# A hybrid decoder step on one Trainium2 core: one of the seven products of the down projection is computed first instead of sixth

## The chip, the cores and the metric

The kernel runs on one core of one Trainium2 chip. The metric is the device time of one execution in microseconds (us). The engines are TensorE (PE, with its weight loads as PEld), VectorE (DVE), ScalarE (ACT), GpSimd (POOL) and SyncE (SP, whose queue issues most DMA transfers). Each engine works through its own queue in order.

## The reference, cut to what matters

One layer of a decoder trunk is computed for 1024 prompt tokens and 8 sample tokens: a gated delta rule, a sliding-window attention, two gates, an output projection, then a feed-forward part, then a last RMSNorm. Only the end of it matters here:

```python
gate = h2 @ lp['w_ffn_gate']
up = h2 @ lp['w_ffn_up']
...
gc = _causal_dwconv(gate_ext, lp['ffn_conv_w'], L) + lp['ffn_conv_b']
x = x + gt2 * ((jax.nn.silu(gc) * up) @ lp['w_ffn_down'])
...
y_prompt = _rmsnorm(xp, final_norm_w)
y_sample = _rmsnorm(xs, final_norm_w)
```

D_MODEL is 1024, D_FF 2816, and everything is float32.

## The kernel before, in words

A float32 product is made of three matmuls in a reduced format: each operand is split in a high and a low part, and `mm3` adds high x high, high x low and low x high (lines L180, L181, L182 in the profile). A split is one ACT instruction (L129, the high part) and one DVE subtraction (L130, the low part).

The down projection multiplies activations (2816 x 1032 tokens) with `w_ffn_down` (2816 x 1024). The method `ffn_down` takes both as 2 x 2 blocks and forms the result from seven block products instead of eight, in Strassen's way. Each product sums over G = 11 pairs of 128 rows; a (product, pair) is called a *step* here, and there are 77, numbered 0 to 76 in the order in which they are computed. A step has 8 tiles of 3 matmuls. Its activations, already added up in pairs, were stored to DRAM (`xd`) by the gate and up stage before. Its weights are made on the spot. The table `made` says how: products 5 and 2 need one 128 x 512 block of the weight (a *light* step), the other five need a sum or difference of two blocks (a *heavy* step). For a heavy step a second block is loaded into a `ws` buffer and POOL adds or subtracts it (L1754).

`fetch(s)` prepares step s: loads on SP's queue (L1750 the first block, L1753 the second, L1755 the activations) into one of five staging buffers (three named `raw`, two halves of `bmh0`), POOL's L1754 for a heavy step, then the split into one of 13 operand buffers. Their names run in the order of the list `tags`, so that steps 0, 13, 26, 39 stand in `bmh2`, steps 1, 14, 27, 40 in `bml0`, and so on. A staging buffer is free again when the DVE half of the split is done; an operand buffer when the matmuls of the step 13 places earlier are done. Fetches 18 to 23 also load a slice of the residual x (L1769).

After the last step of each product except the last product, its eight tiles are copied from their PSUM banks by ACT (`take`, L1782): a *block of copies*, six in all, behind steps 10, 21, 32, 43, 54 and 65. The next product's first matmul into a bank has to wait for that bank's copy. DVE then adds the copied tiles to x with a gate (`add_gated`, L1471, with L1475 and L1476 for the sample tokens): to two places each for products 5, 3, 1 and 2 (16 additions), to one for products 4 and 7 (8 additions), as the table `home` says. The last product, 6, goes tile by tile, and the final RMSNorm (`norm_rows`) is woven into it; it transposes finished columns of x on PE (L190) and squares them on ACT (L1865).

The order of the products is the tuple `chains`; products in one inner tuple share their PSUM accumulation. The program is emitted in this order and a scheduler then sets each engine's queue, by priorities and by its own estimate of times; the queues are fixed when the kernel runs.

Of the kernel before, what the change touches and what calls it, by code (L numbers as in the profile page):

```python
# [64 lines left out]
class Step:  # L65
# [1659 lines left out]
    def ffn_down(self, pool, psum):  # L1725
# [4 lines left out]
        made = {5: (2, (1, 1)), 3: (5, (0, 1), (1, 1), ALU.subtract), 4: (6, (1, 0), (0, 0), ALU.subtract),  # L1730
                7: (4, (1, 0), (1, 1), ALU.add), 1: (0, (0, 0), (1, 1), ALU.add), 2: (1, (0, 0)),
                6: (3, (0, 0), (0, 1), ALU.add)}
        chains = ((5, 3), (4, 7), (1,), (2,), (6,))
        home = {5: ((0, 0, -1), (1, 1, -1)), 3: ((1, 0, 1), (1, 1, 1)), 4: ((0, 1, 1),), 7: ((0, 0, 1),),
                1: ((0, 0, 1), (1, 1, 1)), 2: ((0, 1, 1), (1, 1, -1)), 6: ((1, 1, 1),)}
        steps = [(i, g) for c in chains for i in c for g in range(G)]
# [320 lines left out]
```

## Time and profile before

| | |
|---|---|
| runs shown | 2100.24, 2102.01, 4988.29 us (median 2102.01) |
| profiled execution | 2099.13 us, span 2097.4 us |
| mean granted TensorE clock | 0.983 |
| PE busy | 2027.4 us (97%) |
| DVE, ACT, POOL busy | 1362.2, 902.8, 520.2 us |
| DMA over the span | 275.75 MB, 131 GB/s |
| blocks of copies start at | 1880.7, 1912.2, 1950.5, 1984.6, 2014.6, 2046.2 us |

Times inside the execution count from the start of the span. The time from one block of copies to the next is called a stretch. In rows of a timeline a bracket at the end gives the idle time of the engine before the instruction and what ended it. In the table of stretches the columns are the busy times of PE, PEld, DVE, ACT and POOL with instruction counts, the granted TensorE clock, the DMA engines' busy share and GB/s.

### The profile page before, as it was taken

The numbers are of one execution on the slowest core, as the hardware profiler recorded it, in microseconds if no ns is written. First come the engines' busy times: TensorE is split into PE (matmuls) and PEld (weight loads), VectorE is DVE, ScalarE is ACT, GpSimd is POOL, SyncE is SP. The second block draws the span as 40 slices with busy tenths as digits, with TensorE's granted clock in tenths as the row PEclk, the third lists the DMA queues.
The fourth block names the chain that finished last, engine by engine and source line by source line (L and its number), as shares of the span: only waits on it lengthen the run. The fifth ranks groups of instructions, "written<-read, shape, count | busy, mean of one in ns | idle before, by whom it ended". The sixth has DMA issues, their size and how long they took to land.

```text
span 2097.4 us, 41330 instructions
## 1 busy us (share of the span) xinstructions
PE 2027.4 (97%) x16245; PEld 1924.1 (92%) x16245; DVE 1362.2 (65%) x2733; ACT 902.8 (43%) x2233; POOL 520.2 (25%) x594
## 2 busy tenths in 40 slices
PE   7999999999999999989999999999999999999998
PEld 3987778799999999989988999999999999999898
DVE  4756667564736647566554575479876776778875
ACT  3665545433333342442442452245544544544543
POOL 1000000021321211201211000004556556445530
PEclk8999999899999999999999999999999999999999
DMA  7246344152232312312266774413333333487972
GB/s 270 88 140 213 127 148 140 39 147 62 74 83 55 81 58 70 84 36 70 63 193 188 251 230 134 139 58 93 99 97 112 96 97 92 137 295 272 310 233 84
DMA packets 301887, 275.75 MB, mean 131 GB/s; under 512 B 59730, under 2 KB 248111, under 8 KB 301676
## 3 DMA queue, kind: packets, MB, share of 16 engines
q1 hardware_dynamic: 295852, 252.22, 39.2%
q0 software_dynamic: 5552, 20.37, 2.8%
q8 instruction: 127, 2.08, 0.4%
q14 instruction: 68, 0.56, 0.1%
q10 hardware_dynamic: 288, 0.52, 0.1%
HBM read 212.93 MB, written 62.51 MB: 131 GB/s over the span
## 4 chain that ended last, share of the span: by engine, by line
PE 77%; DMA 8%; DVE 6%; ACT 3%; issue 1%; SPq 1%; POOL 1%; DVEq 0%; POOLq 0%; ACTq 0%
PE mm L180 18%; PE mm L181 17%; PE mm L182 17%; PE wv L180 2%; PE wv L182 2%; PE wv L181 2%; PE pv L653 2%; DMA ws<-in_w_ffn_down_dram 1%; PE wy L180 1%; PE wy L182 1%; PE wy L181 1%; DMA raw<-in_w_ffn_down_dram 1%; PE pt L190 1%; PE tp L190 1%; PE sc L615 1%
## 5 line engine op out<-in xcount | busy, mean ns | idle before, releaser
L180 PE MATMUL mm<-b1h,wh 128*128 128x384 f32 (+1 forms) x1520 | 499.0, 330 | 4.9 <-ACT gt L1293 1.8
L181 PE MATMUL mm<-b1l,wh 128*128 128x384 f32 (+1 forms) x1520 | 491.0, 324 | 0.0
L182 PE MATMUL mm<-b1h,wl 128*128 128x384 f32 (+1 forms) x1520 | 490.6, 325 | 0.0
L180 PEld LDWEIGHTS mm<-b1h,wh 128*128 128x128 f32 x1520 | 287.9, 190 | 15.2 <-issue 5.8
L181 PEld LDWEIGHTS mm<-b1l,wh 128*128 128x128 f32 x1520 | 288.0, 190 | 5.4 <-issue 4.3
L182 PEld LDWEIGHTS mm<-b1h,wl 128*128 128x128 f32 x1520 | 287.3, 189 | 3.2 <-issue 2.3
L129 ACT ACTIVATE wh<-raw 128x1024 fp32r<-128x1024 f32 x83 | 87.0, 1048 | 118.5 <-PE mm L181 72.1
L130 DVE TENSOR_TENSOR wl<-raw,wh 128x1024 fp32r<-128x1024 f32 x82 | 101.2, 1235 | 53.6 <-ACT wh L129 52.5
L181 PE MATMUL mm<-pk,w 128*128 128x260 f32 (+1 forms) x440 | 124.9, 284 | 1.1 <-DVE pk L130 1.1
L180 PE MATMUL mm<-pk,w 128*128 128x260 f32 (+1 forms) x440 | 124.8, 284 | 0.0
L182 PE MATMUL mm<-pk,w 128*128 128x260 f32 (+1 forms) x440 | 124.6, 284 | 0.0
L130 DVE TENSOR_TENSOR w<-ws,w 128x512 fp32r<-128x512 f32 x88 | 79.4, 902 | 38.3 <-ACT w L129 38.1
L1625 ACT COPY bml<-mm 128x256 f32<-128x256 f32 (+1 forms) x132 | 48.9, 371 | 100.2 <-PE mm L182 97.1
L180 PE MATMUL mm<-bmh,w 128*128 128x260 f32 (+1 forms) x320 | 90.3, 282 | 0.0
L182 PE MATMUL mm<-bmh,w 128*128 128x260 f32 (+1 forms) x320 | 90.1, 282 | 0.0
L1680 DVE SCALAR_TENSOR_TENSOR fa<-fz,fcw,fa 128x512 f32<-128x512 f32 x88 | 75.0, 873 | 18.3 <-ACT fa L1678 18.0
L180 PE MATMUL mm<-b2h,wh 128*128 128x384 f32 (+1 forms) x256 | 83.3, 328 | 2.5 <-ACT wh L129 2.1
L181 PEld LDWEIGHTS mm<-pk,w 128*128 128x128 f32 x440 | 83.3, 189 | 1.3 <-DVE pk L130 1.3
L181 PE MATMUL mm<-b2l,wh 128*128 128x384 f32 (+1 forms) x256 | 83.6, 327 | 0.4 <-DVE b2l L130 0.4
L180 PEld LDWEIGHTS mm<-pk,w 128*128 128x128 f32 x440 | 83.3, 189 | 0.2 <-ACT bml L1625 0.2
L182 PEld LDWEIGHTS mm<-pk,w 128*128 128x128 f32 x440 | 83.5, 190 | 0.0
L182 PE MATMUL mm<-b2h,wl 128*128 128x384 f32 (+1 forms) x256 | 82.7, 325 | 0.0
(649 smaller groups left out, 5920.6 us busy)
## 6 DMA issues: line engine op xcount, KB each, us to landing
raw<-in_w_in_dram SPq DMA_DIRECT2D x60, 512.0 KB, 4.0
ws<-in_w_ffn_down_dram SPq DMA_DIRECT2D x55, 256.0 KB, 5.4
raw<-xd SPq DMA_DIRECT2D x47, 258.0 KB, 5.3
raw<-in_w_ffn_down_dram SPq DMA_DIRECT2D x47, 256.0 KB, 4.2
raw<-in_w_ffn_gate_dram SPq DMA_DIRECT2D x22, 512.0 KB, 3.8
raw<-in_w_ffn_up_dram SPq DMA_DIRECT2D x22, 512.0 KB
qst<-in_w_mod_dram SPq DMA_DIRECT2D x16, 512.0 KB, 7.8
raw<-in_w_mod_dram SPq DMA_DIRECT2D x16, 512.0 KB, 6.2
```

Of the source, the lines that this page charges most:

```text
L129: self.nc.scalar.activation(hi, x, AF.Copy)
L130: (eng or self.nc.vector).tensor_tensor(lo, x, hi.bitcast(F32), op=ALU.subtract)
L180: mm(ps, whi, xhi, start=first, stop=False, **kw)
L181: mm(ps, whi, xlo, start=False, stop=False, **kw)
L182: self.last_mm = mm(ps, wlo, xhi, start=False, stop=last, **kw).ins
L190: self.nc.tensor.transpose(out, in_, self.ident[:p, :p])
L615: self.scored = nc.tensor.matmul(sc[:, r, 256 - w:256], q, KH[:, lo:lo + w], start=True, stop=False)
L653: nc.tensor.matmul(pv[64 * r:64 * r + 64], V[:, n - back, ch], ps[:, r::2, :], start=back == 0, stop=back == (n > 0))
L1625: self.last_copy = nc.scalar.copy(r[p, i], x[p])
L1680: nc.vector.scalar_tensor_tensor(ai[:, c:e], zi[:, j + c:j + e], col(j), ai[:, c:e], op0=ALU.mult, op1=ALU.add)
```

## The change

One line changes, the order of the products:

```diff
-        chains = ((5, 3), (4, 7), (1,), (2,), (6,))
+        chains = ((2,), (5, 3), (4, 7), (1,), (6,))
```

Product 2 formerly held steps 55 to 65 and now holds 0 to 10; products 5, 3, 4, 7 and 1 each come 11 steps later; product 6 stays last. Both light products now stand in front: steps 0 to 21 are light and 22 to 76 heavy. Before, steps 0 to 10 and 55 to 65 were light.

ACT, third block of copies (behind step 32). `mm`, `wv`, `wy` and `nr` are the PSUM banks. Before:

```order
L129 ACTIVATE bmh3_2912_22043<-bmh0_2910_22037 128x1028
L129 ACTIVATE bmh2_2914_22077<-bmh0_2910_22037 128x1028
L1782 COPY bml3_2336_15623<-mm_2885_21876 128x256
L1782 COPY bml3_2336_15623<-wv_2886_21877 128x260
L129 ACTIVATE bml0_2917_22112<-raw_2915_22106 128x1028
L1782 COPY bml3_2336_15623<-wy_2887_21878 128x256
L1782 COPY bml3_2336_15623<-mm_2888_21879 128x260
```

Now:

```order
L129 ACTIVATE bml0_2910_22091<-raw_2908_22085 128x1028
L129 ACTIVATE bml2_2914_22129<-raw_2912_22123 128x1028
L129 ACTIVATE bmh1_2918_22167<-raw_2916_22161 128x1028
L1782 COPY bml3_2336_15623<-mm_2840_21446 128x256
L1782 COPY bml3_2336_15623<-wv_2841_21447 128x260
L1782 COPY bml3_2336_15623<-wy_2842_21448 128x256
```

Before, the split of step 39 (`bmh2`) was the last one ahead of the copies and step 40's (`bml0`) stood between them; now the splits of steps 40, 41 and 42 (`bml0`, `bml2`, `bmh1`) stand ahead as well. The second block moved the same way (steps 27, 28 and 29 are now ahead of it), and so did the fourth (53, 54, 55). The first has step 16 ahead instead of 15; the fifth and sixth have the same steps ahead as before, 64 and 75.

POOL, the first weight differences of the down projection. Before:

```order
L1720 DMA xd_2197_14347<-r_2337_15624 128x5x260
L1754 TENSOR_TENSOR raw_2822_21113<-raw_2822_21113,ws_2823_21115 128x512
L1754 TENSOR_TENSOR raw_2825_21122<-raw_2825_21122,ws_2826_21124 128x512
L1765 TENSOR_SCALAR less_2809_21079<-mT_125 128x72
L1754 TENSOR_TENSOR bmh0_2828_21155<-bmh0_2828_21155,ws_2829_21157 128x512
L1754 TENSOR_TENSOR bmh0_2828_21155<-bmh0_2828_21155,ws_2831_21189 128x512
```

Now:

```order
L1720 DMA xd_2197_14347<-r_2337_15624 128x5x260
L1765 TENSOR_SCALAR less_2809_21079<-mT_125 128x72
L1754 TENSOR_TENSOR bmh0_2853_21471<-bmh0_2853_21471,ws_2854_21473 128x512
L1754 TENSOR_TENSOR bmh0_2853_21471<-bmh0_2853_21471,ws_2856_21506 128x512
L1754 TENSOR_TENSOR raw_2850_21461<-raw_2850_21461,ws_2851_21463 128x512
L1754 TENSOR_TENSOR raw_2858_21537<-raw_2858_21537,ws_2859_21539 128x512
```

Before, the first one was made for step 11 (`raw_2822`), then 12, 13, 14; now the first is for step 23 (half of `bmh0_2853`), then 24, 22, 25. On SP's queue the three `ws` loads that stand far ahead serve these steps.

DVE, behind the splits for the third block of copies; the names `x1_` are slices of x. Before:

```order
L130 TENSOR_TENSOR bmh3_2912_22043<-bmh0_2910_22037,bmh3_2912_22043 128x1028
L130 TENSOR_TENSOR bmh2_2914_22077<-bmh0_2910_22037,bmh2_2914_22077 128x1028
L1471 SCALAR_TENSOR_TENSOR x1_0_2334_15618<-bml3_2336_15623,mT_125,x1_0_2334_15618 128x256
L1471 SCALAR_TENSOR_TENSOR x1_0_2334_15618<-bml3_2336_15623,mT_125,x1_0_2334_15618 128x252
L1475 TENSOR_TENSOR gtmp_2942_22399<-bml3_2336_15623,mT_125 128x8
L1476 TENSOR_TENSOR x1_0_2334_15618<-x1_0_2334_15618,gtmp_2942_22399 128x8
L130 TENSOR_TENSOR bml0_2917_22112<-raw_2915_22106,bml0_2917_22112 128x1028
```

Now:

```order
L130 TENSOR_TENSOR bmh1_2918_22167<-raw_2916_22161,bmh1_2918_22167 128x1028
L1471 SCALAR_TENSOR_TENSOR x1_4_2812_21083<-bml3_2336_15623,mT_125,x1_4_2812_21083 128x256 x2
L1471 SCALAR_TENSOR_TENSOR x1_4_2812_21083<-bml3_2336_15623,mT_125,x1_4_2812_21083 128x260
L1471 SCALAR_TENSOR_TENSOR x1_4_2812_21083<-bml3_2336_15623,mT_125,x1_4_2812_21083 128x252
L1475 TENSOR_TENSOR gtmp_2954_22525<-bml3_2336_15623,mT_125 128x8
L1471 SCALAR_TENSOR_TENSOR x1_5_2787_21033<-bml3_2336_15623,mT_125,x1_5_2787_21033 128x256 x2
L1471 SCALAR_TENSOR_TENSOR x1_5_2787_21033<-bml3_2336_15623,mT_125,x1_5_2787_21033 128x260
```

Before, eight additions of product 4 follow here, with splits between them; now sixteen of product 3 follow (a row with x2 stands for two) ahead of the next split.

## The prediction

> **What bounds the kernel now.** I read the page's first table, then the stretches of the down projection, then the timelines of PE, ACT and DVE there.
>
> ```profile
> PE 2027.4 (97%) x16245; PEld 1924.1 (92%) x16245; DVE 1362.2 (65%) x2733; ACT 902.8 (43%) x2233; POOL 520.2 (25%) x594
> ```
>
> PE works 97% of the span, so an edit that leaves its matmuls alone can only win or lose the idle time of PE where the edit acts. In the stretches below (from one block of eight copies to the next; columns PE, PEld, DVE, ACT, POOL, granted clock, DMA share, GB/s) PE has idle time in one place, between 1943.5 and 1950.4, and loses clock behind it.
>
> ```profile
> 1881.00:1912.00 31.00, 31.00 (x263) 31.00 (x262) 25.68 (x35) 13.86 (x19) 18.20 (x11) 1.00 0.90 317
> 1912.00:1943.50 31.50, 31.50 (x266) 31.50 (x266) 28.54 (x35) 13.12 (x18) 17.42 (x11) 1.00 0.76 259
> 1943.50:1950.40 6.90, 2.59 (x22) 2.38 (x20) 4.75 (x3) 3.04 (x3) 3.77 (x4) 0.93 1.00 350
> 1950.40:1984.60 34.20, 33.73 (x263) 33.73 (x264) 26.25 (x29) 15.96 (x22) 20.67 (x13) 0.91 0.91 305
> 1984.60:2014.60 30.00, 29.82 (x249) 29.40 (x248) 20.77 (x22) 14.61 (x21) 6.10 (x4) 1.00 0.77 256
> 2014.60:2046.20 31.60, 31.60 (x268) 31.60 (x267) 25.42 (x35) 14.29 (x20) 17.35 (x9) 1.00 0.65 216
> ```
>
> ```profile
> 1945.69 0.28 PE L181 MATMUL nr<-pk 128*128 128x260 f32 x1
> 1945.81 0.28 PE L182 MATMUL nr<-pk 128*128 128x260 f32 x1
> 1950.87 0.58 PE L180 MATMUL mm<-pk 128*128 128x256 f32 x1 [4.78 <-ACT bml L1782]
> 1951.25 0.41 PE L181 MATMUL mm<-pk 128*128 128x256 f32 x1
> 1951.46 0.41 PE L182 MATMUL mm<-pk 128*128 128x256 f32 x1
> ...
> 1988.52 0.39 PE L180 MATMUL wy<-bml 128*128 128x260 f32 x1 [0.15 <-ACT bml L1782]
> ```
>
> Matmuls start 0.12 us apart, so a product (264 of them) takes 31.2 us of PE. The stall of 4.78 us stands between the third and the fourth product and waits for ACT's copy of the first bank. Afterwards starts are 0.21 apart until 1956.2, some 26 of them: 26 x 0.097 = 2.5 us more. This boundary costs 7.3 us; the next one costs about 0.5 with its slow first matmuls.
>
> Why was ACT late? Its rows show it:
>
> ```profile
> 1880.73 0.37 ACT L1782 COPY bml<-mm 128x256 f32<-128x256 f32 x1 [5.75 <-PE mm L182]
> ...
> 1881.76 1.06 ACT L129 ACTIVATE bmh<-raw 128x1028 fp32r<-128x1028 f32 x1
> ...
> 1910.90 1.07 ACT L129 ACTIVATE bmh<-raw 128x1028 fp32r<-128x1028 f32 x1 [1.17 <-POOL raw L1754]
> 1912.19 0.37 ACT L1782 COPY bml<-mm 128x256 f32<-128x256 f32 x1 [0.23 <-PE mm L182]
> ...
> 1939.26 1.06 ACT L129 ACTIVATE pk<-raw 128x1028 fp32r<-128x1028 f32 x1 [1.17 <-POOL raw L1754]
> 1941.49 1.07 ACT L129 ACTIVATE pk<-raw 128x1028 fp32r<-128x1028 f32 x1 [1.17 <-POOL raw L1754]
> 1943.73 1.07 ACT L129 ACTIVATE pk<-raw 128x1028 fp32r<-128x1028 f32 x1 [1.17 <-POOL raw L1754]
> 1946.02 1.06 ACT L129 ACTIVATE bmh<-bmh 128x1028 fp32r<-128x1028 f32 x1 [1.22 <-POOL bmh L1754]
> 1949.50 1.06 ACT L129 ACTIVATE bmh<-bmh 128x1028 fp32r<-128x1028 f32 x1 [2.41 <-POOL bmh L1754]
> 1950.46 0.35 ACT L1782 COPY bml<-mm 128x256 f32<-128x256 f32 x1
> ...
> 1983.63 1.07 ACT L129 ACTIVATE bmh<-raw 128x1028 fp32r<-128x1028 f32 x1 [1.19 <-POOL raw L1754]
> 1984.60 0.35 ACT L1782 COPY bml<-mm 128x256 f32<-128x256 f32 x1
> ...
> 2014.64 0.37 ACT L1782 COPY bml<-mm 128x256 f32<-128x256 f32 x1 [3.89 <-PE mm L182]
> ...
> 2043.85 1.06 ACT L129 ACTIVATE pk<-raw 128x1028 fp32r<-128x1028 f32 x1 [2.44 <-POOL raw L1754]
> 2046.18 0.37 ACT L1782 COPY bml<-mm 128x256 f32<-128x256 f32 x1 [1.27 <-PE mm L182]
> ```
>
> ACT works in order. The copies of step 32 stand behind the split of step 39, and that split waits for POOL's subtraction of two weight blocks. Heavy steps (two blocks) come at best every 2.24 us (1939.26, 1941.49, 1943.73, 1946.02). PE's 2.84 us a step would cover this, but DVE's additions to x1 come in one burst after each block of copies:
>
> ```profile
> 1886.08 5.33 DVE L1471 SCALAR_TENSOR_TENSOR x<-bml,less,x 128x256 f32<-128x256 f32 x8
> 1920.81 6.39 DVE L1471 SCALAR_TENSOR_TENSOR x<-bml,mT,x 128x256 f32<-128x256 f32 x8
> 2016.72 1.67 DVE L1471 SCALAR_TENSOR_TENSOR x<-bml,mT,x 128x256 f32<-128x256 f32 x4
> 2003.09 2.44 DVE L130 TENSOR_TENSOR pk<-raw,pk 128x1028 fp32r<-128x1028 f32 x2
> ```
>
> ```profile
> L1754 POOL TENSOR_TENSOR raw<-raw,ws x33: 1265/1471/3742, 1860.2 to 2044.2; 128x512 f32<-128x512 f32 x33
> ```
>
> One addition takes 0.42 us where POOL is quiet (2016.72) and 0.67 to 0.80 where POOL subtracts (1886.08, 1920.81); POOL's subtraction ranges from 1.27 to 3.74 us. The two slow each other, the five staging buffers stay full meanwhile, and loads stop. So a stretch is priced by its heavy steps and its additions:
> - 13 heavy splits and 16 additions, started without a reserve: 1912.19 to 1950.46, 38.3 us.
> - 11 heavy splits and 16 additions, started with full buffers: 1881.76 to 1911.97, 30.2 us.
> - 13 heavy and 8 additions: 1950.46 to 1984.60, 34.1 us.
> - 1 light, 10 heavy, 16 additions, with full buffers: 2014.64 to 2044.91, 30.3 us.
> A light split costs DVE 1.22 us (2003.09).
>
> The Trainium skill (SBUF — State Buffer, "Who interferes with whom") says that a VectorE instruction with two SBUF inputs and a GpSimd instruction that reads SBUF exclude each other for a whole instruction. By that rule heavy work and additions simply add up, which agrees with 0.80 against 0.42 us; it speaks against a change that puts heavy steps and additions together, as this one does between the third and the fourth block.
>
> **The change part by part.** Totals stay: 1848 matmuls, 55 heavy and 22 light steps, 48 copies, the same DMAs on SP's queue. What moves is 11 light steps, each with one 256 KB weight load and one load from xd, and each without a POOL subtraction, from places 55–65 to 0–10; the other light product goes from 0–10 to 11–21. POOL's first subtraction is then step 22's group, not step 11. Additions to x1 per stretch, formerly 16, 16, 8, 8, 16 in the five stretches between blocks, become 16, 16, 16, 8, 8, since the moved product has two destinations and so have products 5 and 3.
>
> *Up to the first block of copies:* PE never waits there now, and ACT idles 5.75 us before it. Lighter splits make that idle time longer. The lead cannot be kept, because ACT's next split stands behind the copies, as the built order has it: it has done step 16, formerly 15. Worth 0; with a cover of 5.75 us it also costs 0.
>
> *First to second block:* steps 17–29: 5 light, 8 heavy, 16 additions. From the row with full buffers: 30.2 - 3 x 2.24 + 5 x 1.22 = 29.6. From the one without: 38.3 - 5 x (2.24 - 1.22) = 33.2. PE gives 31.5, and since eight tiles are finished one behind the other, the first copy may be some 2.2 us late before PE waits. I take the middle, 31.4: no stall, and no reserve either. Ends: 0 and 1 us.
>
> *Second to third block:* steps 30–42: 13 heavy, 16 additions. Without a reserve 38.3, as in the row of the same count; with one 30.2 + 2 x 2.24 = 34.7. I take 38.3, since the stretch ahead leaves nothing over. That is the 7.3 us of before again: no difference. Ends: 34.7 would leave 1 us of stall, a gain of 6.3; one microsecond handed on from the stretch ahead costs 1.
>
> *Third to fourth block:* steps 43–55: 13 heavy and now 16 additions, not 8. 38.3 against 34.1: 4.2 us later than the one that just fitted. So PE stalls 4.2 us and loses another 2.5 to slow matmuls: +6.7. Ends: 34.7 is 0.6 late, which the 2.2 us of cover hides (0); a stretch that also finds DVE behind from the additions of the last one adds perhaps 3 (+9.7).
>
> The Trainium skill (TensorE: Matmul & The Clock Gate, "Part 1: The HAM clock gate") states that the slow clock comes after an idle window of about 3.4 us. The 4.78 us stall with slow starts and the 0.15 us one without agree; by the rule a stall under 3.4 us would cost its own length alone, here 4.2 + 2.5 stays, but a 2 us stall would cost 2, not 4.5.
>
> *Fourth to fifth:* 9 heavy, 8 additions: 34.1 - 4 x 2.24 = 25.1, under 31.2, no stall. The 0.5 us at the old fourth boundary is inside the +6.7. *Fifth to sixth:* 11 heavy, 8 additions: 34.1 - 2 x 2.24 = 29.6, under 31.2: no stall (end: 1).
>
> *The tail:* product 1's additions, now last, touch the first quarter of the tokens, which the final norm transposes first; product 2's did not.
>
> ```profile
> 2046.59 0.48 DVE L1471 SCALAR_TENSOR_TENSOR x<-bml,mT,x 128x256 f32<-128x256 f32 x1
> ...
> 2052.50 0.60 PE L190 MATMUL wv<-ident,x 128*128 128x128 f32 x4
> ```
>
> The thirteenth addition is the last that matters: 2046.59 + 13 x 0.42 = 2052.1, ahead of 2052.50, and its transpose was put 12 matmuls later. Worth 0, at worst 1.
>
> **Sum:** 0 + 0 + 0 + 6.7 + 0 + 0 = +6.7 us on the profiled 2099.13 (span 2097.4), 2105.8. The runs shown are 2100.24 and 2102.01 beside one of 4988; their middle, 2101.1, lies 2.0 above the profiled one, so I forecast 2108.
>
> **The rivals.** *The lead is kept* (not slower): if 29.6 holds in the first stretch, buffers are full at the second block, the next takes 34.7 and the third as well. The stall of 7.3 shrinks to about 1 and none follows: 2101.1 - 6.5 = 2095. For it: eleven early subtractions are gone, and DMA falls from 317 GB/s there. Against it: the five buffers hold light steps while DVE adds, so no heavy step is staged when the burst ends. *The stall only moves*: one of the two stretches runs at 35 and the other at 38.3; 2099 to 2103, say 2101. *A third stall* (slower): the first heavy loads start when DVE's burst ends near 1889, and 8 heavy steps at 2.9 us (38.3 / 13) need 24 us, to 1913 and beyond, with steps 17–21 between. This decides from 33.7 us on; the second block stalls 2 to 3 us, the next stretches inherit it: +6.7 + 3 + 5 = 2116. *No effect*: were copies not behind splits on ACT, order would not matter; the 4.78 us row speaks against it.
>
> **How the numbers follow.** Forecast, by itself 2104 to 2111 (+3 to +10 us): 0.38. Lead kept: 0.24. Moved only: 0.18. Third stall: 0.18. No effect: 0.02. The range reaches from 2095 (lead kept) to 2118 (third stall and the tail's 1). Faster or slower by over 2% (42 us, about what a measurement of this kernel can tell from no change) would take six stalls of 7 us, one at every boundary: 0.02 for slower; for faster there are only 8 us to win: 0.01.
>
> **What would show it.** Right: PE idle 4 to 6 us behind ACT L1782 at the third and the fourth boundary, each followed by starts 0.21 apart, none at the others; DVE bursts at 0.7 to 0.8 us an addition. Wrong: no stall at the third boundary (lead kept), or one at the second (third stall), or PE waiting in the tail for x1. ACT's idle time before the first copies must grow beyond 5.75 us.

## The result and the profile after

The changed kernel takes 2105.5 us (median of 15 runs, 2101.7 to 2109.78) beside 2100.19 us for the kernel before on the same chip (15 runs): the ratio is 1.0028, with a 95% interval of 1.002 to 1.0036. By the bound of 2% this is no change; as a difference of 0.3% it is resolved, and it is a loss. The forecast was 2108.0 us, with a range of 2095 to 2118. The profiled execution takes 2106.4 us, 7.3 more than that of before.

PE's timeline of the changed kernel has three waits of more than 0.3 us from the first block of copies to the end. (Columns: start, duration, instruction, and in brackets the idle time before it and what ended it.)

```profile
1949.44 0.58 PE L180 MATMUL mm<-pk 128*128 128x256 f32 x1 [4.72 <-ACT bml L1782]
1989.97 0.58 PE L180 MATMUL mm<-bml 128*128 128x256 f32 x1 [6.29 <-ACT bml L1782]
2096.20 0.80 PE L190 MATMUL wy<-ident,x 128*128 128x128 f32 x2 [0.98 <-ACT ws L1865]
```

The stall at the third boundary is still there, a second one stands at the fourth, and both wait for ACT's copy. The wait of 0.98 in the tail is the same as before. ACT's timeline gives the starts of the six blocks of copies, and here the split ahead of three of them:

```profile
1877.34 1.06 ACT L129 ACTIVATE bmh<-raw 128x1028 fp32r<-128x1028 f32 x1 [5.48 <-DMA raw<-xd]
1879.01 0.38 ACT L1782 COPY bml<-mm 128x256 f32<-128x256 f32 x1 [0.60 <-PE mm L182]
...
1912.50 0.35 ACT L1782 COPY bml<-mm 128x256 f32<-128x256 f32 x1
...
1948.07 1.06 ACT L129 ACTIVATE bmh<-raw 128x1028 fp32r<-128x1028 f32 x1 [0.17 <-POOL raw L1754]
1949.04 0.35 ACT L1782 COPY bml<-mm 128x256 f32<-128x256 f32 x1
...
1988.60 1.06 ACT L129 ACTIVATE bmh<-raw 128x1028 fp32r<-128x1028 f32 x1 [0.80 <-POOL raw L1754]
1989.56 0.35 ACT L1782 COPY bml<-mm 128x256 f32<-128x256 f32 x1
...
2021.89 0.37 ACT L1782 COPY bml<-mm 128x256 f32<-128x256 f32 x1 [4.95 <-PE mm L182]
...
2053.39 0.37 ACT L1782 COPY bml<-mm 128x256 f32<-128x256 f32 x1 [2.49 <-PE mm L182]
```

A bracket that names PE means that ACT was there first; the second, third and fourth block have no such bracket, so there ACT was late. At the third and fourth the copies start the moment the splits of steps 42 and 55 are done. The stretches are 33.5, 36.5, 40.5, 32.3 and 31.5 us long, where before they were 31.5, 38.3, 34.1, 30.0 and 31.5. In the table of stretches (columns as before) the 7 us ahead of both blocks have little PE work, a DMA share near 1, and the stretches behind them a granted clock near 0.92:

```profile
1879.00:1912.50 33.50, 33.50 (x283) 33.50 (x282) 28.24 (x45) 16.52 (x22) 14.21 (x8) 1.00 0.87 297
1912.50:1942.50 30.00, 30.00 (x251) 29.81 (x250) 27.50 (x35) 12.83 (x19) 19.42 (x11) 1.00 0.77 252
1942.50:1949.40 6.90, 2.23 (x19) 2.02 (x17) 4.60 (x4) 3.46 (x5) 3.60 (x3) 0.92 0.96 332
1949.40:1983.00 33.60, 33.56 (x260) 33.56 (x261) 28.81 (x35) 12.59 (x17) 22.94 (x11) 0.92 0.73 247
1983.00:1990.00 7.00, 0.71 (x7) 0.50 (x5) 4.67 (x4) 3.52 (x5) 4.50 (x4) 0.70 1.01 361
1990.00:2021.90 31.90, 31.90 (x245) 31.90 (x246) 22.79 (x26) 11.35 (x17) 17.95 (x12) 0.91 0.79 264
```

The balance of the two profiled executions: the first block starts 1.7 us earlier, from the first to the sixth it takes 174.4 us instead of 165.4, and from the sixth to the end 51.3 instead of 51.2. That is -1.7 + 9.0 + 0.1 = 7.3 us. Of the 9.0, stalls make 6.1 (11.0 instead of 4.9) and the second period of slow clock about 2.5.

The timeline of DVE in the burst behind the third block shows how additions go:

```profile
1950.31 2.70 DVE L1471 SCALAR_TENSOR_TENSOR x<-bml,mT,x 128x256 f32<-128x256 f32 x4
1952.93 0.15 DVE L1475 TENSOR_TENSOR gtmp<-bml,mT 128x8 f32<-128x8 f32 x1
1953.01 1.66 DVE L1471 SCALAR_TENSOR_TENSOR x<-bml,mT,x 128x256 f32<-128x256 f32 x4
...
1956.25 1.26 DVE L1476 TENSOR_TENSOR x<-x,gtmp 128x8 f32<-128x8 f32 x1
1957.44 1.66 DVE L1471 SCALAR_TENSOR_TENSOR x<-bml,mT,x 128x256 f32<-128x256 f32 x4
```

Most of them take 0.42 us (1.66 for four). Some instruction in between takes about 1.1 us more, and it need not be a large one: an addition of 128 x 8 values takes 0.15 us or 1.26.

### The profile page after: what moved, and what is told of

Read it like the earlier page. It is cut to its first block, busy times and chain, and to the rows that moved or that the text cites. A ratio compares the mean times of both kernels' runs of the same rounds, so it can differ in the third digit from the quotient of the medians.

```text
span 2104.7 us, 41320 instructions
## 1 busy us (share of the span) xinstructions
PE 2029.8 (96%) x16245; PEld 1926.4 (92%) x16245; DVE 1364.8 (65%) x2733; ACT 902.9 (43%) x2233; POOL 528.4 (25%) x594
## 4 chain that ended last, share of the span: by engine, by line
PE 78%; DMA 7%; DVE 7%; ACT 3%; issue 1%; SPq 1%; POOL 1%; DVEq 0%; POOLq 0%; ACTq 0%
PE mm L180 18%; PE mm L181 17%; PE mm L182 17%; PE wv L180 2%; PE wv L182 2%; PE wv L181 2%; PE wy L182 1%; PE wy L180 1%; PE wy L181 1%; PE pv L653 1%; PE tp L190 1%; PE mm L264 1%; PE pt L190 1%; PE tp L905 1%; PE tp L906 1%
## 5 line engine op out<-in xcount | busy, mean ns | idle before, releaser
L130 DVE TENSOR_TENSOR wl<-raw,wh 128x1024 fp32r<-128x1024 f32 x82 | 101.5, 1238 | 53.7 <-ACT wh L129 52.7
L130 DVE TENSOR_TENSOR w<-ws,w 128x512 fp32r<-128x512 f32 x88 | 79.8, 907 | 38.0 <-ACT w L129 37.9
```

The source lines that it names most:

```text
L130: (eng or self.nc.vector).tensor_tensor(lo, x, hi.bitcast(F32), op=ALU.subtract)
```

## The experiments

The **theory** was that the copies are late because they stand on ACT behind splits of steps far ahead, and that those splits are late because heavy steps and additions share the time of a stretch (theory A: DVE and POOL exclude each other). **Rivals**: PE's operands are late in any case; the loads set the pace (theory B); the burst of additions starves the loads (theory C). Times below stand against the kernel before, run on the same chip.

**1. Fewer splits ahead of the copies.** In both kernels,

```diff
-                        fetch_to(s + len(tags))
+                        fetch_to(s + len(tags) if s >= 55 else min(s + len(tags), s - g + G + 7))
```

On the changed kernel:

> The changed kernel with one more edit: up to step 54 the splits may run at most six steps past the end of the product being computed, not ten, so that on ACT the copies of the third block stand behind the split of step 39 and those of the fourth behind step 50, not 42 and 55. The computation is the same. Theory (the copies are late only because they queue on ACT behind splits that are far ahead and late): the stalls of 4.72 and 6.29 us at the third and fourth block both vanish, and with them about 2 x 2.5 us of slow clock; time about 2105.5 - 16 = 2090 us, and every block but the first starts 31.2 to 32 us after the one before. Rival (the operands themselves are late): the two stalls go from the bank's copy to the operands of the next product (PE waits for a split, at some step behind the boundary), and the time stays at 2102 to 2106.

Measured: 2098.56 us, ratio 1.0007 (0.9996 to 1.0018). ACT's timeline for the third and fourth block, and PE's waits:

```profile
1940.72 0.35 ACT L1782 COPY bml<-mm 128x256 f32<-128x256 f32 x1
1972.71 0.35 ACT L1782 COPY bml<-mm 128x256 f32<-128x256 f32 x1
```

```profile
2007.47 0.39 PE L180 MATMUL mm<-bmh 128*128 128x256 f32 x1 [1.81 <-ACT bml L1782]
2045.87 0.58 PE L180 MATMUL mm<-bml 128*128 128x260 f32 x1 [6.61 <-ACT bml L1782]
```

The stretches up to the fourth block are 31.4, 31.8 and 32.0 us: with 11 or 12 splits in a stretch both stalls are gone, and no operand was late in their place. So the wait is the place of the copies in ACT's queue; the first rival falls. The gain, by the ratios 0.2% or 4 us where I expected 15, is mostly lost again at the sixth block: the limit ends at step 55, so that 14 heavy splits stand between the fifth and the sixth, 38.4 us and a stall of 6.61. The fifth block, 1.81 us late, I had not expected: 11 heavy splits and 8 additions in 34.4 us. The loads had paused there behind the burst (the row has a DMA share of 0.16), and ACT then waited for POOL, which waited for its loads.

```profile
1982.00:1987.00 5.00, 5.00 (x44) 5.00 (x43) 4.78 (x5) 1.07 (x1) 5.00 (x2) 1.00 0.16 59
```

On the kernel before:

> The same limit of six steps on the kernel before (order 5, 3, 4, 7, 1, 2, 6). Theory: its one stall (4.78 us with 2.5 of slow clock) vanishes, about 2100.2 - 7 = 2093 us, and it then differs from the limited changed kernel by less than 3 us: without copies behind late splits the order of the products hardly matters. Rival (operands late): no gain, 2098 to 2101, and the changed order with the limit stays about 5 us slower than this one.

Measured: 2097.96 us, ratio 1.0003 (0.9991 to 1.0014), and the stall at the third boundary stayed (5.13 us, stretch 38.6). This was a slip of mine: the kernel before has the split of step 39 ahead of the third block anyway, and 26 ahead of the second, so the limit left 13 heavy splits in that stretch. It fits the theory, but tests nothing.

**2. Other places for the light steps.**

```diff
-        chains = ((2,), (5, 3), (4, 7), (1,), (6,))
+        chains = ((5, 3), (2,), (4, 7), (1,), (6,))
```

> The order 5, 3, 2, 4, 7, 1, 6: the light product 2 third, no other edit. Light steps are then 0 to 10 and 22 to 32; stretches hold 5 heavy + 8 light steps with 16 additions, 3 light + 10 heavy with 16, 13 heavy with 16, 9 heavy with 8, 11 heavy with 8. Theory (a stretch is priced by its heavy steps and additions): the second block is on time, the third is up to 2 us late (no more than a short stall), the fourth is the late one (13 heavy + 16 additions, 36.5 to 40.5 us by the two such stretches of the changed kernel) and stalls 3 to 7 us; time 2097 to 2103. Rival (the place of the third block as such is late, whatever steps stand there): a stall of 4 to 5 us at the third block.

Measured: 2098.98 us, ratio 1.0008 (0.9997 to 1.0018); stalls of 1.63 at the third and 5.96 at the fourth boundary, stretches of 31.8, 34.9, 37.7, 32.0 and 31.5. All as the theory had it.

```diff
-        chains = ((2,), (5, 3), (4, 7), (1,), (6,))
+        chains = ((4, 7), (5, 3), (2,), (1,), (6,))
```

> The order 4, 7, 5, 3, 2, 1, 6: light steps are 22 to 32 and 44 to 54, so that they are split where DVE has 16 additions, and heavy ones where it has 8. Stretches: 5 heavy + 8 light with 8 additions, 3 light + 10 heavy with 8, 2 heavy + 11 light with 16, 9 heavy with 16, 11 heavy with 16. Theory: no stall at the second to the sixth block, which saves the 7.3 us of the kernel before; but the first two products are heavy, so POOL has 17 subtractions to make before the first block, where it still adds up activations: this may cost 0 to 10 us at the beginning of the down projection. Time 2093 to 2103. Rival (the load traffic paces the heavy steps, not their sharing with additions): a stall of 4 us or more at the third block, since there the 10 heavy steps also need two loads each.

Measured: 2098.2 us, ratio 1.0007 (0.9994 to 1.0021). Behind the first block every stretch is 31.4 or 31.5 us long, without a stall; PE's waits all stand before:

```profile
1845.43 0.39 PE L180 MATMUL mm<-pk,w 128*128 128x256 f32 x1 [1.21 <-ACT bml L1625]
1850.45 0.39 PE L180 MATMUL wv<-pk,w 128*128 128x256 f32 x1 [1.66 <-DVE bml L1700]
1888.73 0.58 PE L180 MATMUL mm<-pk 128*128 128x256 f32 x1 [5.60 <-ACT bml L1782]
```

Light steps among the additions keep the stretches in time, as the theory prices them, and heavy steps in front cost their time ahead of the first block: the three waits add up to 8.5 us, and the kernel before has none of them.

```diff
-        chains = ((2,), (5, 3), (4, 7), (1,), (6,))
+        chains = ((5, 3), (1,), (2,), (4, 7), (6,))
```

> The order 5, 3, 1, 2, 4, 7, 6: light steps are 0 to 10 and 33 to 43; stretches hold 13 heavy steps with 16 additions (started with full buffers), 3 heavy + 10 light with 16, 1 light + 12 heavy with 16 (started with full buffers again), 9 heavy with 16, 11 heavy with 8. Theory (a stretch is late only where about 13 heavy steps meet 16 additions without a light product before them): no stall at any block, each block 31.2 to 32 us after the one before, time of the kernel before less 7.3, about 2091 us, the ratio 0.996 to 0.9975. Rival (whichever stretch first has 13 heavy steps and 16 additions is late): a stall of 4 us or more at the second block or at the fourth, and a time of 2096 to 2101.

Measured: 2105.35 us, ratio 1.0037 (1.0025 to 1.005), and stalls at the third and the fifth boundary:

```profile
1948.88 0.58 PE L180 MATMUL mm<-pk 128*128 128x256 f32 x1 [5.05 <-ACT bml L1782]
2019.72 0.58 PE L180 MATMUL mm<-bmh 128*128 128x256 f32 x1 [5.46 <-ACT bml L1782]
```

My expectation failed, and the rival's places were wrong too. I had counted the steps of each stretch as they are in the changed kernel. The queue of this order has 16 splits between the second and the third block (steps 27 to 42: 6 heavy, 10 light; 38.6 us) and 13 heavy ones between the fourth and the fifth (steps 54 to 66, with 16 additions; 38.9 us). PE uses up 11 steps in a stretch. How many splits the queue puts between two blocks matters as much as how heavy they are.

The first of these two stretches also shows a second way to be late, which the price by heavy steps and additions does not cover. POOL's last subtraction in it ends at 1924.1 and DVE's burst at 1925.1. The loads had stood still behind the burst (a DMA share of 0.20 in the row), ACT then idled 8.05 us for activations, and nine of the ten light splits waited for a load:

```profile
1925.00:1930.00 5.00, 5.00 (x44) 5.00 (x44) 5.00 (x10) 0.18 (x1) 0.00 (x0) 1.00 0.20 62
1933.23 1.07 ACT L129 ACTIVATE pk<-bmh 128x1028 fp32r<-128x1028 f32 x1 [8.05 <-DMA bmh<-xd]
```

**3. Taking away one cost at a time** in the stretch between the third and the fourth block. Additions first:

```diff
-        home = {5: ((0, 0, -1), (1, 1, -1)), 3: ((1, 0, 1), (1, 1, 1)), 4: ((0, 1, 1),), 7: ((0, 0, 1),),
+        home = {5: ((0, 0, -1), (1, 1, -1)), 3: ((1, 1, 1),), 4: ((0, 1, 1),), 7: ((0, 0, 1),),
```

> The changed kernel with product 3 added to one place instead of two (its additions to the other quarter are left out): 8 additions instead of 16 in the stretch from the third to the fourth block, nothing else moved. Theory (additions and heavy steps share the time of the stretch): the stretch falls from 40.5 us to 34 to 36 us, the stall of 6.29 us at the fourth block to 0 to 2.5 us, and the time by 5 to 8 us to about 2098. Rival (loads alone pace the heavy steps): 13 heavy steps have the same loads, the stretch stays at 39 to 41 us and the stall above 5 us.

Then the loads (for product 7 POOL adds the two blocks; the texts call this a subtraction too):

```diff
-                other = self.t(self.pw, [P, 512], "ws", bufs=3)
-                nc.sync.dma_start(other, src[1])
+                other = raw[:, n:] if i == 7 else self.t(self.pw, [P, 512], "ws", bufs=3)
+                if i != 7:
+                    nc.sync.dma_start(other, src[1])
```

> The changed kernel with the second weight load of product 7 (steps 44 to 54) left out; POOL still subtracts, a block from itself. Of the 13 heavy steps between the third and the fourth block 11 then load 514 KB instead of 770. Theory A (DVE and POOL in each other's way set the pace): the stretch stays at 39 to 41 us and the stall above 5 us. Theory B (the loads set the pace, 770 KB a step at about 350 GB/s being 2.2 us): 11 x 0.73 = 8 us less, the stretch falls to 32 or 33 us and the stall vanishes.

Then the subtractions:

```diff
-                nc.gpsimd.tensor_tensor(raw[:, n:], raw[:, n:], other, op=src[2])
+                if i != 7:
+                    nc.gpsimd.tensor_tensor(raw[:, n:], raw[:, n:], other, op=src[2])
```

> The changed kernel with POOL's subtraction for product 7 (steps 44 to 54) left out; both loads are still made. Theory A (DVE and POOL in each other's way): additions fall to 0.42 us throughout in that stretch, which ends 8 us or more sooner, 31 to 33 us, without a stall. Theory B (loads): the stretch stays at 38 to 41 us, since 770 KB are loaded for each step as before. Between them, 35 to 37 us: the burst of additions holds back the buffers and the loads have to catch up, so that both count.

One row of the stretches for each, in this order (columns as before):

```profile
1950.30:1985.20 34.90, 34.45 (x264) 34.25 (x264) 29.74 (x30) 15.88 (x22) 21.40 (x14) 0.91 0.87 306
```

```profile
1951.70:1986.70 35.00, 33.53 (x264) 33.32 (x264) 29.92 (x38) 15.83 (x23) 18.00 (x14) 0.94 0.64 215
```

```profile
1952.00:1983.80 31.80, 31.44 (x251) 31.44 (x252) 24.44 (x38) 15.67 (x23) 2.86 (x3) 0.95 0.95 339
```

| left out | stretch | stall at the fourth boundary | median, ratio |
|---|---|---|---|
| nothing | 40.5 us | 6.29 us | 2105.5, 1.0028 (1.002 to 1.0036) |
| 8 additions | 35.0 | 0.51 | 2101.32, 1.0016 (1.0005 to 1.0026) |
| 11 second loads | 35.0 | 1.44 | 2103.78, 1.0031 (1.0019 to 1.0042) |
| 11 subtractions | 31.8 | below 0.3 | 2098.42, 1.0005 (0.9995 to 1.0014) |

With half the additions and without the subtractions the stretch came out as theory A had it (34 to 36 and 31 to 33 us) and not as B had it (38 us or more). Without the second loads it lies between the two: loads count (5.5 us, where B said 8), but with the DMA engines busy only 0.64 of the time the stretch is still 35 us long. So neither alone holds. Without the subtractions it falls to PE's pace with every load in place, and DVE's small additions (from 1952 to 1984 us, the changed kernel first; busy us and mean ns) are short:

```profile
L1476 DVE TENSOR_TENSOR x<-x,gtmp 128x8 f32<-128x8 f32 x4 | 2.8, 710 | 0.0
L1476 DVE TENSOR_TENSOR x<-x,gtmp 128x8 f32<-128x8 f32 x4 | 0.5, 148 | 0.0
```

The times fall by less than the stretches: by the ratios 2.5 us with half the additions, where I expected 5 to 8, nothing without the second loads, 4.8 us without the subtractions. The kernel with fewer loads stalls 2.46 us at the sixth boundary, where the changed kernel does not, and 1.21 us at the second, ahead of its own edit:

```profile
1914.73 0.38 PE L180 MATMUL mm<-pk 128*128 128x256 f32 x1 [1.21 <-ACT bml L1783]
```

**4. Spreading the additions.** In both kernels,

```diff
-                                add(*(waiting[0] or waiting[1]).pop(0))
+                                with self.tc.issue_after(halves[min(s + 6, 75)].ins):
+                                    add(*(waiting[0] or waiting[1]).pop(0))
```

where `halves[s]` is the DVE subtraction of the split of step s. On the changed kernel:

> The changed kernel, with each pair of additions held on DVE until the low half of a split is done (the pair made in step s stands behind the split of step s + 6), so that DVE has two additions between two splits in place of sixteen in a row. ACT's order of splits and copies is the same as in the changed kernel but for one split. The computation is the same. Theory C (the burst itself is what delays: while it lasts, the five staging buffers stay full and the loads stand still, DMA share 0.1 to 0.6 behind it): the stretches from the second to the fourth block fall from 36.5 and 40.5 to 33 to 35 us, the stalls of 4.72 and 6.29 to 0 to 2.5 each, time 2092 to 2098. Theory A (additions and subtractions exclude each other and the time of a stretch is their sum, in whatever order): the stretches stay at 36 to 40 us, both stalls above 4 us, time 2103 to 2107.

Measured: 2103.15 us, ratio 1.0031 (1.0019 to 1.0044), stretches of 34.7, 37.8 and 37.0 us, and three stalls whose sum, 11.15 us, is that of the changed kernel (11.01):

```profile
1917.42 0.39 PE L180 MATMUL mm<-pk 128*128 128x256 f32 x1 [1.11 <-ACT bml L1782]
1955.20 0.58 PE L180 MATMUL mm<-pk 128*128 128x256 f32 x1 [6.12 <-ACT bml L1782]
1992.18 0.48 PE L180 MATMUL mm<-bml 128*128 128x256 f32 x1 [3.92 <-ACT bml L1782]
```

Theory C's forecast (33 to 35 us, stalls of 0 to 2.5) falls for these stretches: the DMA engines are hardly busier than in the changed kernel (0.83 beside 0.82 from 1878 to 1990 us). What the spreading won in one place it lost on DVE. Most pairs of additions now take 1.9 us, where a pair in the middle of a burst took 0.83 (half of 1.66). DVE's timeline:

```profile
1931.26 1.92 DVE L1471 SCALAR_TENSOR_TENSOR x<-bml,less,x 128x256 f32<-128x256 f32 x2
1933.10 2.32 DVE L130 TENSOR_TENSOR pk<-bmh,pk 128x1028 fp32r<-128x1028 f32 x1
1935.34 1.90 DVE L1471 SCALAR_TENSOR_TENSOR x<-bml,less,x 128x256 f32<-128x256 f32 x2
```

All 48 additions from 1878 to 1990 us (DVE's busy time with L1471, granted clock, DMA share, GB/s), in the changed kernel and with the spreading:

```profile
1878.00:1990.00 112.00, 25.13 (x48) 0.95 0.82 277
1878.00:1990.00 112.00, 39.52 (x48) 0.97 0.83 282
```

By these times an addition that stands between two splits meets a POOL instruction more often than one in a row of additions. The splits (L130) take 52.0 us instead of 58.6 there (39 and 40 of them).

On the kernel before:

> The same spreading on the kernel before. Theory C: its one stall (4.78 us) falls below 2 us, time 2090 to 2094, ratio 0.996 to 0.998. Theory A: the stretch from the second to the third block stays at 37 to 39 us, the time within 2 us of the kernel before. In both kernels: no stall that was not there before.

Measured: 2103.49 us, ratio 1.0035 (1.0022 to 1.0048): slower. The stall at the third boundary was gone, but PE waited 0.39 and 2.48 us for the low half of a split behind the second block, and 4.50 us at the fourth. The stretch from the second to the third block stayed at 37.7 us, as theory A had it; that no stall would come where there was none before was wrong in both kernels.

**5. The subtraction on DVE instead of POOL.** If the two exclude each other anyway, the faster engine should do it:

```diff
-                nc.gpsimd.tensor_tensor(raw[:, n:], raw[:, n:], other, op=src[2])
+                nc.vector.tensor_tensor(raw[:, n:], raw[:, n:], other, op=src[2])
```

> The changed kernel with POOL's additions and subtractions of weight blocks (L1754) made by DVE instead; the computation is the same. Theory A (POOL and DVE exclude each other, so that their work adds up as on one engine): DVE needs about 0.6 us for a 128 x 512 subtraction (half of the 1.22 of a 128 x 1028 one) where POOL needs 1.27, and no addition waits for POOL any more. 13 heavy steps and 16 additions then cost 13 x 1.8 + 16 x 0.42 + 8 x 0.15 = 31.3 us in place of 36.5 and 40.5: both stalls fall below 2.5 us, all additions take 0.42 to 0.5, time 2092 to 2098. Rival (POOL's subtractions mostly ran beside DVE's work and cost the stretch little): 13 more instructions on DVE lengthen a stretch by 13 x 0.6 = 8 us, the stalls grow, time 2110 or more. What speaks against a full gain in any case: DVE works in order, and a subtraction that waits for its two loads holds up the additions behind it.

> The same move from POOL to DVE in the kernel before. Theory A: its stall of 4.78 us falls below 2 us, time 5 to 8 us under the kernel before, ratio 0.996 to 0.998, and less than 4 us from the changed kernel with the same move. Rival: the stall grows and others come, time above 2105.

Measured: the changed kernel with this move takes 2088.51 us, ratio 0.9956 (0.994 to 0.9971), the kernel before with it 2087.66 us, ratio 0.9948 (0.9934 to 0.9963): both faster than either kernel, by less than the bound of 2%, and not to be told apart. Not one stall over 0.3 us is left at a boundary of either. In the changed kernel ACT is at the third and fourth block ahead of PE:

```profile
1947.49 0.37 ACT L1782 COPY bml<-mm 128x256 f32<-128x256 f32 x1 [1.06 <-PE mm L182]
1978.85 0.37 ACT L1782 COPY bml<-mm 128x256 f32<-128x256 f32 x1 [0.68 <-PE mm L182]
```

The view of single lines (least, median and most ns of one instruction, from 1878 to 2050 us) shows what the exclusion cost DVE. The changed kernel:

```profile
L1476 DVE TENSOR_TENSOR x<-x,gtmp x20: 152/157/1279, 1883.7 to 2000.9; 128x8 f32<-128x8 f32 x20
L130 DVE TENSOR_TENSOR pk<-bmh,pk x14: 1216/1230/2323, 1887.4 to 2047.4; 128x1028 fp32r<-128x1028 f32 x14
```

The same with the subtractions on DVE:

```profile
L1476 DVE TENSOR_TENSOR x<-x,gtmp x21: 158/171/181, 1890.1 to 2047.1; 128x8 f32<-128x8 f32 x21
L130 DVE TENSOR_TENSOR pk<-bmh,pk x14: 1221/1228/1246, 1893.8 to 2034.8; 128x1028 fp32r<-128x1028 f32 x14
```

The most now lies close to the least. The rival (13 more instructions lengthen the stretch) falls, and theory A holds: where DVE and POOL no longer meet, PE waits at no boundary. The built order helped at one place, since 12 splits stand between the second and the third block instead of 13; between the third and the fourth there are 13 as before, and that stretch takes 31.4 us instead of 40.5. Not separated is how much comes from the end of the exclusion and how much from the shorter instruction. The gain was larger than I had put it, although a subtraction took 0.69 us and not 0.6: the changed kernel with the move lies 9.0 us under the kernel before (2097.49 on that chip), where I had 0 to 6. By the two ratios, 0.9956 and 1.0028, the move is worth about 15 us to it, what its two stalls (11.0) and the slow clock behind them (some 5) had cost.

## Why the prediction was right, and where not

**The stall at the third boundary stays** (forecast 4.8): 4.72. Right, for the reason given.

**A stall at the fourth boundary** (forecast 4.2, with 2.5 of slow clock behind it): 6.29, with about 2.5. The place, the sign and the mechanism were right, and the experiments show it: the stall goes with fewer splits ahead of the copies and without the subtractions, and little of it is left with half the additions (0.51) or without the second loads (1.44). The price by heavy steps and additions holds the loads as well, which the prediction did not set apart. The size of this term was 2.1 us short. The price it rests on, 38.3 us for 13 heavy steps and 16 additions, came from one row. The changed kernel alone gave 36.5 and 40.5, and other such stretches in the experiments 37.2 to 38.9: the price is good as a mean, to about 2 us.

**First to second block** (forecast 31.4, ends 29.6 and 33.2): 33.5 us. The middle was wrong and the upper end right; the 2.2 us of cover hid it, and PE worked through. So "no stall" was right, and the reserve that the rival of a kept lead needed was not there. That this execution had no stall there was in part luck: the run without second loads, the same kernel up to that point, had one of 1.21 us, and the spread additions brought one of 1.11.

**Fourth to sixth block and the tail**: no stall, and 0.1 us, as forecast.

**Signs that were wrong.** ACT's idle time before the first copies was to grow beyond 5.75 us. It fell to 0.60. The idle time had moved one split ahead: 5.48 us before step 16's, for its load of activations. And additions take no 0.7 to 0.8 us in a burst: the mean hid two kinds, 0.42 us, and 1.1 more for the one that meets a POOL instruction.

**What the sum got for nothing.** The first block came 1.7 us early. The three kernels of part 3, which are the changed kernel up to there, had it at 1880.1, 1880.4 and 1882.6 us, so this much differs from one execution to the next. It cancelled most of the 2.1 that the fourth stall was short. The forecast for one profiled execution, +6.7 beside a measured +7.3, is closer than its terms. The medians differ by 5.3 us. The 2.0 us put on top of the profiled time, from two runs, were too much: the median of the kernel before lies 1.1 above its profiled execution.

The Trainium skill (SBUF — State Buffer, "Who interferes with whom") states that a VectorE instruction with two SBUF inputs and a GpSimd instruction that reads SBUF exclude each other; the 128 x 8 addition of 0.15 or 1.28 us, never more than 0.18 once POOL is quiet, agrees with it. For the clock (TensorE: Matmul & The Clock Gate, "Part 1: The HAM clock gate") it gives an idle window of about 3.4 us; here single stalls up to 2.46 us were followed by a clock of 1.00, and those from 3.92 us on by one of 0.50 to 0.75 over the next 6 us. Two waits close together, 0.39 and 2.48 us in the kernel before with spread additions, were followed by 0.52 from 1916 to 1922 us. The rows behind the stalls of 1.44 and 2.46 us (without second loads) and of 3.92 us (spread additions):

```profile
1987.00:1993.00 6.00, 5.91 (x49) 5.91 (x50) 6.00 (x11) 3.99 (x10) 2.41 (x2) 1.00 0.55 184
2053.20:2059.00 5.80, 4.75 (x38) 4.51 (x38) 5.80 (x13) 3.03 (x9) 2.13 (x1) 1.00 0.00 0
```

```profile
1992.00:1998.00 6.00, 5.82 (x36) 5.83 (x37) 6.00 (x10) 3.26 (x10) 3.40 (x2) 0.72 0.67 215
```

Open is how loads and exclusion share the 35 us of the stretch without second loads, how much the stop of the loads behind a burst costs by itself, and where the microseconds ahead of the first block arise.

## What to carry to other kernels

Where a short copy frees what the busiest engine waits for, read in the built order how much work stands ahead of it on its engine and compare with what is used up meanwhile: PE used up 11 steps in a stretch here, and 13 heavy ones with 16 additions were late wherever they stood as long as POOL did their subtractions. No order tried was faster than that of the kernel before; the way out was to take the contention away. Before giving work to an idle engine, look whether the least and the most time of a tiny instruction on its neighbour differ by the length of that engine's instructions: then the two may be running in turn, and it is worth trying all of the work on the faster one.

## What the runs showed of the hardware that I had not expected

A DVE instruction of 128 x 8 values took 1.29 us at worst beside POOL's subtractions, more than eight times its 0.15; without them 0.18. The DVE did the same 128 x 512 subtraction in 0.69 us that took POOL 1.27 at best and a mean of 1.8 in the down projection of the changed kernel, so that moving 55 instructions to the engine that was already busier (65% against 25%) took about 10 us off the kernel before and 15 off the changed one.
